# x^T and the branch outputs keep high and low parts side by side, so one 512-column matmul serves both

## The chip, the cores and the metric

The kernel runs on one core of a Trainium2 chip. The metric is the time of one execution in microseconds of device time, the median of three runs. The profile is one execution recorded by the hardware profiler.

## The reference

Two layers of a streaming encoder over 256 tokens (T) of 1024 channels (D). In each layer x passes through four residual steps, each closed by a layer norm:

```
x = LN(a x + 0.5 swiglu_1(x))            swiglu(x) = (silu(x Wg) * (x Wu)) Wd,  2816 hidden columns
x = LN(a x + mixer(x))
x = LN(a x + 0.5 swiglu_2(x))
x = LN(a x + sigmoid(x Wgate + b) * (p Wproj))
```

The mixer projects x once to the inputs of three branches (a recurrent unit RG-LRU, a gated linear attention GLA, a forgetting attention FoX) and to three gates of 1024 columns. Each branch ends in a product of its 512-column output with a branch weight, the three results are gated and added, and a last 1024x1024 product closes the mixer. All of it is float32.

## The kernel before

**Precision.** A float32 product is made of three matmuls of a shorter type (fp32r). Each operand is split in a high part (a ScalarE copy) and a low part (VectorE, the value minus the high part), and the three products high·high, low·high and high·low are summed in one PSUM bank.

**Weights.** 440 pieces of up to 128x1024 are loaded by SP's DMA queue in the order of their use. ScalarE makes `whi` (line 194), VectorE (or GpSimd at some places) makes `wlo` (line 195). Eight pieces, in the feed-forward phases up to 13, are held split, and further ones wait in four raw tiles. A piece is split as soon as one is freed by its last matmul, so the split of a later piece stands on ScalarE's and VectorE's queues behind each unit of work.

**Two kinds of product.** `mm_tok` (lines 288 to 298) holds x^T blocks stationary and moves up to 512 weight columns. `mm_feat` (lines 300 to 310) holds 128x128 of the weights stationary and moves x^T, 256 columns (all tokens): per block one matmul with `XH` on the high weights (line 308), one with `XL` on the high weights (309), one with `XH` on the low weights (310). The output is feature-major, 128 channels by 256 tokens, and two such outputs lie side by side in one bank. A unit of `feat` is 256 columns: two pieces, 16 triples of matmuls. A unit of `branch` has 8 triples, with the branch output `yh`/`yl` moving. Over both layers there are 118 units of `feat` (the first gate chunk of each layer's first feed-forward step counted as one, although it is written out) and 24 of `branch`: 118 x 16 + 24 x 8 = 2080 triples.

**PSUM.** All products take their banks in turn from one pool `ps` of eight 2 KB banks. Who takes a bank waits for the last reader of the tile that had it.

**Order.** Nothing is scheduled at run time: every engine executes its queue in the order in which the program issues it. A feed-forward step runs over 11 chunks of 256 hidden columns: gate unit, silu (ScalarE, from the bank), up unit, product of both (VectorE, from the bank), split into `hh` and `hl`; the down product of a chunk follows two chunks later (`LAG`), and the last two stand at the end. In the mixer the units follow one another while chains of small operations (the recurrent unit, decays, attention) advance one step per unit. Near its start stand, in this order, two units `v` (FoX values, `mm_tok`, copied from their banks by ScalarE at line 553), between them the RG-LRU gates (PE line 667, sigmoids on ScalarE line 671) and `gla_states` (PE line 718). At its end come the third branch's units; each gets its gate factor (VectorE `w<-w,ps`), is added to `mg` and split into `XH` and `XL`, and the closing product (`merge_out`) reads these.

Of the kernel before, what the change touches and what calls it, by code (L numbers as in the profile page):

```python
# [30 lines left out]
# Weight pieces held split: always, and further ones in the feed-forward phases; raw pieces; work tiles.  # L31
# [25 lines left out]
# A group of attention heads starts at every so many units of the merge.  # L57
# [8 lines left out]
def weight_units():  # L66
    """Weight blocks in the order in which the kernel uses them.

    (key, array, index, row 0, rows, column 0, columns, cut): a unit comes in two pieces, cut by rows or by columns."""
# [65 lines left out]
# per-channel vectors of the RG-LRU, feature-major  # L135
# [17 lines left out]
class Weights:  # L153
    """Weight pieces, loaded and split in two float32r parts ahead of their use."""
# [21 lines left out]
    def prefetch(self, n=1, lo=None, cuts=1, between=lambda i: None):  # L176
        """Split up to n more pieces, as far as there is room."""
        for _ in range(n):
            where = self.room()
            if where is None:  # L180
                return False
            key, _, _, _, rows, _, cols, off = PIECES[self.next]
            kt = rows // P
            raw = self.raw.tile([P, PCAP], F32, tag="raw", name=f"raw{self.next}")
            pool = self.extra if where == "extra" else self.main
            hi, lw = (pool.tile([P, PCAP], F32R, tag=x, bufs=R_EXTRA if where == "extra" else R_MAIN, name=f"{x}{self.next}") for x in ("whi", "wlo"))
            hi, lw, raw = (x[:, :kt * cols] for x in (hi, lw, raw))
            src = self.src[off:off + rows * cols].rearrange("(p n) -> p n", p=P)
            m = kt * cols // cuts
            for i in range(cuts):  # L190
                between(i)
                c = slice(i * m, (i + 1) * m)
                self.nc.sync.dma_start(raw[:, c], src[:, c])
                self.nc.scalar.activation(hi[:, c], raw[:, c], AF.Copy)  # L194
                (lo or self.nc.vector).tensor_tensor(out=lw[:, c], in0=raw[:, c], in1=hi[:, c].bitcast(F32), op=ALU.subtract)  # L195
            self.live[key] = [x.rearrange("p (k n) -> p k n", k=kt) for x in (hi, lw)] + [where]
            self.used[where] += 1
            self.next += 1
        return True
# [12 lines left out]
class Chains:  # L212
    """Chains of operations, each a generator, that advance by one step at a time."""
# [11 lines left out]
def build(tc, a, out):  # L225
# [10 lines left out]
    psp = pool("ps", 8, space=PSUM)  # L236
# [8 lines left out]
    def ps():  # L245
        return psp.tile([P, 512], F32, tag="ps", name=nm("ps"))

# [27 lines left out]
    XH = const.tile([P, KD, T], F32R, name="XH")  # L275
    XL = const.tile([P, KD, T], F32R, name="XL")
# [11 lines left out]
    def mm_tok(o, t, w, k0, start, stop, lh=None, ll=None):  # L288
        """o[tokens of tile t, columns] += x^T blocks (stationary) with a piece (moving)."""
        lh, ll = (XH, XL) if lh is None else (lh, ll)  # L290
        hi, lo = w
        kt = hi.shape[1]
        c = slice(t * P, (t + 1) * P)
        for kk in range(kt):
            k = k0 + kk
            TE.matmul(o, lhsT=lh[:, k, c], rhs=hi[:, kk, :], start=start and kk == 0, stop=False)  # L296
            TE.matmul(o, lhsT=lh[:, k, c], rhs=lo[:, kk, :], start=False, stop=False)  # L297
            TE.matmul(o, lhsT=ll[:, k, c], rhs=hi[:, kk, :], start=False, stop=stop and kk == kt - 1)  # L298

    def mm_feat(o, w, col, k0=0, start=True, stop=True, rh=None, rl=None):  # L300
        """o[128 columns of a piece, all tokens] += piece^T (stationary) with x^T (moving)."""
        rh, rl = (XH, XL) if rh is None else (rh, rl)
# [3 lines left out]
        for kk in range(kt):  # L306
            k = k0 + kk
            TE.matmul(o, lhsT=hi[:, kk, c], rhs=rh[:, k, :], start=start and kk == 0, stop=False)  # L308
            TE.matmul(o, lhsT=hi[:, kk, c], rhs=rl[:, k, :], start=False, stop=False)  # L309
            TE.matmul(o, lhsT=lo[:, kk, c], rhs=rh[:, k, :], start=False, stop=stop and kk == kt - 1)  # L310

    def feat(key):
        """256 columns of a product, feature-major, of a unit cut by columns."""
        o = ps()
        for i in range(2):
            mm_feat(o[:, i * T:(i + 1) * T], W.get(key, i), 0)
            W.free(key, i)
        return o

# [11 lines left out]
    class Norm:  # L331
        """Layer norm of tile t of 2 ALPHA x + an addend that comes in column blocks."""
# [14 lines left out]
        def finish(self, gb, cuts=((0, 512), (512, 512)), last=False):  # L347
            """Normalizes; returns what turns the halves feature-major."""
# [25 lines left out]
    def to_feat(y, hi, lo):  # L374
        """hi, lo [128, 4, 128] of the transpose of y [128, 512]."""
# [5 lines left out]
    def steps(work_list, at=(), turn=(), ahead="", inserts={}):  # L381
        """Runs the steps: after step at[n], turn[n]; after step i, a piece split ahead by engine ahead[i]."""
# [11 lines left out]
    def ffn(l, f, ln, hp, turn):  # L394
# [19 lines left out]
        if not first:  # L414
            ht(0), ht(1)

            def up_tok(t, c):
                st = {}

                def step(x, i):  # L420
                    if not st:
                        st["o"] = ps()
# [27 lines left out]
        for c in range(0 if first else 2, NCH):  # L450
            if first and c == 0:
                og = [ps() for _ in range(2)]
                for i in range(2):
                    w = W.get((l, f, "g", c), i)
                    for k in range(4):
                        for j in range(2):
                            mm_feat(og[j][:, :T], [x[:, k:k + 1, :] for x in w], j * P, 4 * i + k, i == 0 and k == 0, i == 1 and k == 3)
                    W.free((l, f, "g", c), i)
            else:
                og = feat((l, f, "g", c))  # L460
            s = work()
            while late:
                late.pop()()
            if isinstance(og, list):
                for j in range(2):
                    S.activation(s[:, j * T:(j + 1) * T], og[j][:, :T], AF.Silu)
            else:
                S.activation(s, og, AF.Silu)
# [30 lines left out]
    def mixer(l, turn):  # L499
# [15 lines left out]
        # columns that are needed token-major  # L515
        acc = {}

        def b_piece(g, t, h, i):
            n = PB[g + 1] - PB[g]
            if (g, t) not in acc:  # L520
                acc[g, t] = ps()
# [33 lines left out]
        def abs_log1p(z, n):  # L555
            """Room for log(sigmoid(z)) = min(z, 0) - log(1 + exp(-|z|)), and that logarithm."""
# [6 lines left out]
        # Each step of these chains needs what earlier steps made, so that no engine waits long.  # L563
        # GLA: decayed keys and chunk decays
# [37 lines left out]
        # FoX: cumulative log forget gates, in three exact bfloat16 parts, transposed  # L602
# [32 lines left out]
        def yt():  # L635
            return [mt([P, 4, T], F32R, x, 2) for x in ("yh", "yl")]

        # RG-LRU
# [21 lines left out]
        def lru(i):  # L660
# [18 lines left out]
            # 1 - a^2 = -tanh(log a) (1 + a^2)  # L679
# [10 lines left out]
            hi, lo = (flat(x[:, 2 * i:2 * i + 2, :]) for x in ya)  # L690
            S.activation(hi, xc, AF.Copy)
            yield
            tt(lo, xc, hi.bitcast(F32), ALU.subtract)

        # head by head, the rows of the other head of the pair zero
# [11 lines left out]
        # GLA: states and outputs  # L707
# [26 lines left out]
        def gla_gate():  # L734
            """silu(r) * norm_g, without its factor of one half."""
# [11 lines left out]
        def gla_out():  # L747
# [25 lines left out]
            for t in range(2):  # L773
                to_feat(sq[t], yb[0][:, :, t * P:(t + 1) * P], yb[1][:, :, t * P:(t + 1) * P])
                yield

        # FoX: attention, in groups of heads that share a PSUM bank
        def fox_attend(t, g):
# [41 lines left out]
            if (g + 1) * nh == NH:  # L820
                if t == 0:
                    fox["y"] = yt()
                split(*(x[:, :, tk] for x in fox["y"]), oy.rearrange("p (h c) -> p h c", h=4))

        # merge: gates (1 + tanh(x / 2)), twice the sigmoid; the factor of two goes into the norm
# [3 lines left out]
        def gate(b, i):  # L829
            o = feat((l, f"gt{b}", i))  # L830
            s = work()
            S.activation(s, o, AF.Tanh, scale=0.5)
            ss[i] = s

        def merge(b, h, q, o):
# [10 lines left out]
            if b == 2:  # L846
                yield
                f = 4 * h + 2 * q
                split(flat(XH[:, f:f + 2, :]), flat(XL[:, f:f + 2, :]), m)

        def branch(b, h, y):
            for q in range(2):
                key = (l, "br", b, h)
                o = ps()
                w = W.get(key, q)
                for j in range(2):
                    mm_feat(o[:, js[j]], w, j * P, rh=y[0], rl=y[1])
                chains.add(merge(b, h, q, o))
# [75 lines left out]
    def ple(l, turn, last):  # L934
# [4 lines left out]
        for t in range(2):  # L939
            for n in range(2):  # L940
                o = ps()
# [34 lines left out]
        def last_step(q):  # L976
            """The last 512 columns in two blocks, so that little is left after the last product."""
# [32 lines left out]
    def lru_constants():  # L1010
        # -8 softplus(-lambda), with log1p(e) = 2 atanh(e / (2 + e))
# [22 lines left out]
    def x_part(k):  # L1034
        s = raws[k // 4][:, (k % 4) * 256:(k % 4 + 2) * 256]
        load(s, a["xT"][:, k * 256:(k + 2) * 256])
        split(flat(XH[:, k:k + 2, :]), flat(XL[:, k:k + 2, :]), s)
# [82 lines left out]
```

## Time and profile before

| | |
|---|---|
| median of 3 runs | 1336.01 us (1334.59 to 1336.84) |
| span of the profiled execution | 1332.8 us |
| mean granted TensorE clock | 0.996 |
| PE busy | 1308.0 us, 98% |
| VectorE busy | 834.6 us, 63% |
| ScalarE busy | 663.3 us, 50% |
| GpSimd busy | 106.2 us, 8% |
| DMA | 246.17 MB, mean 185 GB/s |

The span is that of the recorded instructions; the time of a run is some 3.2 us longer. A row of the timeline gives the start and the duration in us, engine, line, operation, the tiles out<-in, the shape, how many instructions it groups, and in brackets the idle time before it and what ended it. Matmuls are pipelined: their recorded durations overlap, so what one costs is read from the distance between starts.

### The profile page before, as it was taken

Reading aid. Unit: us, or ns where it says so; the run is one execution under the profiler, and the core shown is the slowest. Engines: PE = TensorE matmul, PEld = TensorE weight load, DVE = VectorE, ACT = ScalarE, POOL = GpSimd, SP = SyncE. Lnnn points to the kernel's source line nnn. Section 1 sums busy time; section 2 is a strip of 40 time slices with the busy share of each in tenths; the row PEclk is TensorE's granted clock in tenths of the full one; section 3 lists DMA queues with packets and bytes.
Section 4 is the critical chain, followed back from the end, with each engine's and each line's share of the span. In section 5 each row is a group of like instructions: output and inputs, shape, how many; then the busy total and the mean of one; then the engine's idle time right before and its main releaser. Section 6 shows DMA issues by size and latency. Waiting matters only on the chain. (4 is left out here: it accounts for less than half of the span.)

```text
span 1332.8 us, 22835 instructions
## 1 busy us (share of the span) xinstructions
PE 1308.0 (98%) x9492; PEld 1231.9 (92%) x9492; DVE 834.6 (63%) x992; ACT 663.3 (50%) x869; POOL 106.2 (8%) x69
## 2 busy tenths in 40 slices
PE   8999999999999999999999999999999999999997
PEld 8999999999999999998799999899999989999986
DVE  6665567675657755557775555676755587555576
ACT  6554436965445344454344445279654444444441
POOL 0000001000001400001320000200000022000021
PEclk9999999999999999999999999999999999999998
DMA  8855636445466365574456567454554554656732
GB/s 269 289 198 190 243 127 229 160 159 167 150 190 204 129 193 188 188 239 164 174 191 187 190 185 239 157 184 160 183 160 145 194 187 150 194 188 185 251 128 78
DMA packets 70215, 246.17 MB, mean 185 GB/s; under 512 B 8160, under 2 KB 8672, under 8 KB 70112
## 3 DMA queue, kind: packets, MB, share of 16 engines
q1 hardware_dynamic: 69824, 244.33, 56.6%
q8 instruction: 74, 1.21, 0.4%
q10 hardware_dynamic: 288, 0.39, 0.1%
q14 instruction: 29, 0.24, 0.1%
HBM read 243.64 MB, written 1.05 MB: 184 GB/s over the span
## 5 line engine op out<-in xcount | busy, mean ns | idle before, releaser
L195 DVE TENSOR_TENSOR wlo<-raw,whi 128x1024 fp32r<-128x1024 f32 (+3 forms) x419 | 513.5, 1235 | 393.3 <-ACT whi L194 392.1
L194 ACT ACTIVATE whi<-raw 128x1024 fp32r<-128x1024 f32 (+3 forms) x442 | 459.5, 1047 | 443.8 <-PE ps L309 258.7
L308 PE MATMUL ps<-XH,whi 128*128 128x256 f32 x1888 | 535.1, 283 | 5.7 <-ACT whi L194 5.7
L309 PE MATMUL ps<-XL,whi 128*128 128x256 f32 x1888 | 531.0, 281 | 0.0
L310 PE MATMUL ps<-XH,wlo 128*128 128x256 f32 x1888 | 531.0, 281 | 0.0
L308 PEld LDWEIGHTS ps<-XH,whi 128*128 128x128 f32 x1888 | 357.2, 189 | 8.1 <-ACT whi L194 5.7
L309 PEld LDWEIGHTS ps<-XL,whi 128*128 128x128 f32 x1888 | 357.0, 189 | 1.4
L310 PEld LDWEIGHTS ps<-XH,wlo 128*128 128x128 f32 x1888 | 357.2, 189 | 0.2 <-DVE wlo L195 0.2
L296 PE MATMUL ps<-whi,XH 128*128 128x256 f32 (+3 forms) x488 | 162.3, 333 | 0.0
L297 PE MATMUL ps<-wlo,XH 128*128 128x256 f32 (+3 forms) x488 | 159.2, 326 | 0.0
L298 PE MATMUL ps<-whi,XL 128*128 128x256 f32 (+3 forms) x488 | 158.4, 325 | 0.0
L296 PE MATMUL ps<-whi,hh 128*128 128x512 f32 x368 | 144.5, 393 | 0.0
L298 PE MATMUL ps<-whi,hl 128*128 128x512 f32 x368 | 143.6, 390 | 0.0
L297 PE MATMUL ps<-wlo,hh 128*128 128x512 f32 x368 | 143.4, 390 | 0.0
L298 PEld LDWEIGHTS ps<-whi,XL 128*128 128x128 f32 x488 | 92.1, 189 | 6.6
L296 PEld LDWEIGHTS ps<-whi,XH 128*128 128x128 f32 x488 | 91.9, 188 | 6.8 <-ACT tm L553 0.3
L297 PEld LDWEIGHTS ps<-wlo,XH 128*128 128x128 f32 x488 | 92.3, 189 | 5.9
L298 PEld LDWEIGHTS ps<-whi,hl 128*128 128x128 f32 x368 | 69.1, 188 | 15.0
L297 PEld LDWEIGHTS ps<-wlo,hh 128*128 128x128 f32 x368 | 69.3, 188 | 13.0
L296 PEld LDWEIGHTS ps<-whi,hh 128*128 128x128 f32 x368 | 69.1, 188 | 12.8
L354 POOL TENSOR_TENSOR s<-s,mhalf 128x1 f32<-128x1 f32 x16 | 15.6, 976 | 792.5 <-DVE s L266 792.5
L195 POOL TENSOR_TENSOR wlo<-raw,whi 128x1024 fp32r<-128x1024 f32 (+1 forms) x23 | 58.1, 2534 | 32.9 <-ACT whi L194 29.3
(161 smaller groups left out, 1053.4 us busy)
## 6 DMA issues: line engine op xcount, KB each, us to landing
raw<-in_wu SPq DMA_DIRECT2D x414, 512.0 KB, 4.1
gb<-in_lnp SPq DMA_DIRECT2D x16, 512.0 KB, 6.5
raw<-in_wu SPq DMA_DIRECT2D x16, 436.0 KB, 4.3
raw<-in_wu SPq DMA_DIRECT2D x8, 432.0 KB, 4.5
xr<-in_xT SPq DMA_DIRECT2D x4, 256.0 KB, 4.6
raw<-in_wu SPq DMA_DIRECT2D x4, 256.0 KB, 5.1
XR<-in_x SPq DMA_DIRECT2D x1, 1024.0 KB, 7.0
wa<-in_lru SPq DMA_DIRECT2D x2, 512.0 KB, 3.8
```

What stands on the lines that cost most here:

```text
L194: self.nc.scalar.activation(hi[:, c], raw[:, c], AF.Copy)
L195: (lo or self.nc.vector).tensor_tensor(out=lw[:, c], in0=raw[:, c], in1=hi[:, c].bitcast(F32), op=ALU.subtract)
L296: TE.matmul(o, lhsT=lh[:, k, c], rhs=hi[:, kk, :], start=start and kk == 0, stop=False)
L297: TE.matmul(o, lhsT=lh[:, k, c], rhs=lo[:, kk, :], start=False, stop=False)
L298: TE.matmul(o, lhsT=ll[:, k, c], rhs=hi[:, kk, :], start=False, stop=stop and kk == kt - 1)
L308: TE.matmul(o, lhsT=hi[:, kk, c], rhs=rh[:, k, :], start=start and kk == 0, stop=False)
L309: TE.matmul(o, lhsT=hi[:, kk, c], rhs=rl[:, k, :], start=False, stop=False)
L310: TE.matmul(o, lhsT=lo[:, kk, c], rhs=rh[:, k, :], start=False, stop=stop and kk == kt - 1)
L354: G.tensor_tensor(out=rs, in0=rs, in1=mhalf[:, 0:1], op=ALU.pow)
```

## The change

XH and XL become two views of one tile `XX` [128, 8, 2, 256], and `yh` and `yl` of one tile `y` [128, 4, 2, 256], so that for a block k the high and low parts are 512 columns in a row. `mm_feat` sends both through the high weights in one 512-column matmul; the 256-column matmul with the low weights adds to the second half. The first half of a bank then holds high·high, the second half the two small products. A unit of 256 columns takes two banks (a tile `pp`) in place of one. `summed` adds the halves: ScalarE copies the second halves to SBUF, VectorE adds the first halves. What read the bank before (silu, tanh, the product, the split, the gate factor) reads the sum in SBUF now. The pool `ps` has four banks, and `pp` has two tiles of two.

```diff
-    psp = pool("ps", 8, space=PSUM)
+    psp = pool("ps", 4, space=PSUM)
+    ppp = pool("pp", 2, space=PSUM)
...
-    XH = const.tile([P, KD, T], F32R, name="XH")
-    XL = const.tile([P, KD, T], F32R, name="XL")
+    XX = const.tile([P, KD, 2, T], F32R, name="XX")
+    XH, XL = XX[:, :, 0, :], XX[:, :, 1, :]
...
         for kk in range(kt):
             k = k0 + kk
-            TE.matmul(o, lhsT=hi[:, kk, c], rhs=rh[:, k, :], start=start and kk == 0, stop=False)
-            TE.matmul(o, lhsT=hi[:, kk, c], rhs=rl[:, k, :], start=False, stop=False)
-            TE.matmul(o, lhsT=lo[:, kk, c], rhs=rh[:, k, :], start=False, stop=stop and kk == kt - 1)
+            both = rhs[:, k].rearrange("p s c -> p (s c)")
+            last = stop and kk == kt - 1
+            if not last:
+                TE.matmul(o, lhsT=hi[:, kk, c], rhs=both, start=start and kk == 0, stop=False)
+            TE.matmul(o[:, T:], lhsT=lo[:, kk, c], rhs=rhs[:, k, 0, :], start=False, stop=False)
+            if last:
+                TE.matmul(o, lhsT=hi[:, kk, c], rhs=both, start=False, stop=True)
+
+    def summed(o):
+        s = work()
+        v = s.rearrange("p (j c) -> p j c", j=2)
+        S.activation(v, o[:, :, T:], AF.Copy)
+        tt(v, o[:, :, :T], v, ALU.add)
+        return s
 
     def feat(key):
-        o = ps()
+        o = pp()
         for i in range(2):
-            mm_feat(o[:, i * T:(i + 1) * T], W.get(key, i), 0)
+            mm_feat(o[:, i, :], W.get(key, i), 0)
+            if i:
+                s = summed(o)
             W.free(key, i)
-        return o
+        return s
...
-            S.activation(s, og, AF.Silu)
+            S.activation(s, s, AF.Silu)
...
-                chains.add(merge(b, h, q, o))
+                chains.add(merge(b, h, q, summed(o)))
```

Some other products (the first two chunks' token-major part of a later feed-forward step, two groups of the mixer's token-major columns, the embedding product) take pairs of `pp` banks in place of `ps` banks; their arithmetic is the same.

On ScalarE, around the copies of the first `v` unit (`tm<-ps` at the end of the piece), the queue was this (L658 are the gelus of two `ay` units, L683 and L560 belong to chains):

```order
L560 ACTIVATE w_2598<-w_2598 128x16
L194 ACTIVATE whi_2632<-raw_2631 128x1024
L194 ACTIVATE whi_2662<-raw_2661 128x1024
L658 ACT_TABLE_LOAD
L658 ACTIVATE w_2667<-ps_2606 128x512
L683 ACT_TABLE_LOAD
L683 ACTIVATE w_2498<-w_2498 128x512
L194 ACTIVATE whi_2702<-raw_2701 128x1024
L194 ACTIVATE whi_2732<-raw_2731 128x1024
L553 ACTIVATE tm_2072<-ps_2675 128x256
L553 ACTIVATE tm_2072<-ps_2676 128x256
L671 ACT_TABLE_LOAD
```

The same place of the changed kernel (L681 is the gelu, L706 and L582 the chains, L575 the copies of `v`, L694 the sigmoids):

```order
L582 ACTIVATE w_2258<-w_2258 128x16
L194 ACTIVATE whi_2284<-raw_2283 128x1024
L327 ACTIVATE w_2305<-pp_2266 128x512
L194 ACTIVATE whi_2309<-raw_2308 128x1024
L681 ACT_TABLE_LOAD
L681 ACTIVATE w_2314<-w_2305 128x512
L706 ACT_TABLE_LOAD
L706 ACTIVATE w_2171<-w_2171 128x512
L194 ACTIVATE whi_2349<-raw_2348 128x1024
L194 ACTIVATE whi_2379<-raw_2378 128x1024
L575 ACTIVATE tm_1775<-ps_2322 128x256
L575 ACTIVATE tm_1775<-ps_2323 128x256
```

The copy of the `ay` unit's second halves (L327) is new there; another stands before the first `ay` unit's gelu. On PE the instructions that follow the first `v` unit are the same in both kernels; in the changed one they stand as below, with the semaphores they wait for (L690 the RG-LRU gates, L742 `gla_states`, L301 the second `v` unit):

```order
L690 MATMUL ps_2393<-w_2075,wa_1771 128x256 [waits Activation_49]
L690 MATMUL ps_2396<-w_2075,wa_1771 128x256 [waits Activation_49]
L742 MATMUL ps_2407<-tm_1775,w_2316 64x128 [waits DVE_49,Activation_49]
L742 MATMUL ps_2407<-tm_1775,w_2316 64x128 x3
L742 MATMUL ps_2408<-tm_1775,w_2318 64x128 [waits DVE_49,Activation_49]
L742 MATMUL ps_2408<-tm_1775,w_2318 64x128 x3
L301 MATMUL ps_2437<-whi_2150,XX 128x256 [waits Activation_49]
L301 MATMUL ps_2438<-whi_2150,XX 128x256 [waits Activation_49]
```

With four banks in turn, `ps_2407` and `ps_2408` take the banks of `ps_2322` and `ps_2323` (the first `v` unit), and `ps_2437` and `ps_2438` those of `ps_2393` and `ps_2396`. On VectorE, before the closing product of the mixer, the queue was (L263 the gate factors, `XL<-mg` the low parts that the closing product reads):

```order
L263 SCALAR_TENSOR_TENSOR w_4344<-w_4344,ps_4518 128x512
L195 TENSOR_TENSOR wlo_4547<-raw_4545,whi_4546 128x1024
L260 TENSOR_TENSOR XL<-mg_3426,XH 128x512
L263 SCALAR_TENSOR_TENSOR w_4414<-w_4414,ps_4551 128x512
L195 TENSOR_TENSOR wlo_4582<-raw_4580,whi_4581 128x1024
L260 TENSOR_TENSOR XL<-mg_3426,XH 128x512
L845 TENSOR_TENSOR mg_3677<-mg_3677,w_4414 128x512
```

and is now (`w<-pp,w` are the adds of `summed`):

```order
L264 TENSOR_TENSOR w_3903<-pp_3886,w_3903 128x512
L267 SCALAR_TENSOR_TENSOR w_3737<-w_3737,w_3903 128x512
L195 TENSOR_TENSOR wlo_3910<-raw_3908,whi_3909 128x1024
L264 TENSOR_TENSOR w_3931<-pp_3914,w_3931 128x512
L264 TENSOR_TENSOR XX<-mg_2975,XX 128x2x256
L267 SCALAR_TENSOR_TENSOR w_3793<-w_3793,w_3931 128x512
L195 TENSOR_TENSOR wlo_3940<-raw_3938,whi_3939 128x1024
L264 TENSOR_TENSOR w_3961<-pp_3944,w_3961 128x512
L264 TENSOR_TENSOR XX<-mg_2975,XX 128x2x256
L868 TENSOR_TENSOR mg_3188<-mg_3188,w_3793 128x512
```

One add per branch unit stands ahead of the gate factor and of the split that is due there.

## Rows read from the trace of the kernel before

**Rows 1.** Page, part 1: busy time of each engine, share, instructions.
```profile
PE 1308.0 (98%) x9492; PEld 1231.9 (92%) x9492; DVE 834.6 (63%) x992; ACT 663.3 (50%) x869; POOL 106.2 (8%) x69
```
**Rows 2.** Waits over the whole span: engine, line, releaser, total us, times, longest.
```profile
ACT whi L194 <- PE ps L309: 258.7, 152, 4.0
```
**Rows 3.** Timeline of PE, feed-forward: a down product, then an up unit (256 columns).
```profile
42.66 0.28 PE L310 MATMUL ps<-XH,wlo 128*128 128x256 f32 x1
42.78 0.39 PE L296 MATMUL ps<-whi,hh 128*128 128x512 f32 x1
...
48.01 0.39 PE L298 MATMUL ps<-whi,hl 128*128 128x512 f32 x1
48.23 0.28 PE L308 MATMUL ps<-XH,whi 128*128 128x256 f32 x1
...
98.83 0.28 PE L308 MATMUL ps<-XH,whi 128*128 128x256 f32 x1
...
104.53 0.28 PE L308 MATMUL ps<-XH,whi 128*128 128x256 f32 x1
```
**Rows 4.** Timeline of PE in the closing product of the mixer.
```profile
417.59 0.40 PE L296 MATMUL ps<-whi,XH 128*128 128x512 f32 x1
...
423.90 0.39 PE L296 MATMUL ps<-whi,XH 128*128 128x512 f32 x1
...
425.30 0.39 PE L296 MATMUL ps<-whi,XH 128*128 128x512 f32 x1
```
**Rows 5.** Groups by shape, ScalarE and VectorE: busy us, mean ns, idle before.
```profile
L832 ACT ACTIVATE w<-ps 128x512 f32<-128x512 f32 x24 | 14.0, 582 | 0.0
L260 DVE TENSOR_TENSOR w<-w,ps 128x512 f32<-128x512 f32 x38 | 25.8, 680 | 0.0
```
**Rows 6.** Timeline of PE after the first v unit.
```profile
259.12 1.97 PE L718 MATMUL ps<-tm,w 128*64 128x128 f32 x32
261.02 0.39 PE L296 MATMUL ps<-whi,XH 128*128 128x256 f32 x1
```
**Rows 7.** Timeline of ScalarE, same place.
```profile
238.41 1.28 ACT L671 ACT_TABLE_LOAD   x1
...
258.65 1.99 ACT L194 ACTIVATE whi<-raw 128x1024 fp32r<-128x1024 f32 x2
260.55 0.64 ACT L553 ACTIVATE tm<-ps 128x256 f32<-128x256 f32 x2
...
262.50 1.57 ACT L671 ACTIVATE w<-ps,vec 128x256 f32<-128x256 f32 x4
```
**Rows 8.** Timeline of PE at a norm, then windows (PE to POOL busy, PEclk, DMA).
```profile
660.86 1.11 PE L378 MATMUL ps<-cf,XR 128*128 128x128 f32 x4 [2.56 <-DVE XR L263]
660.00:665.00 5.00, 4.14 (x17) 3.52 (x18) 4.24 (x7) 2.90 (x4) 1.45 (x2) 0.66 0.33 105
```
**Rows 9.** Timeline near the start: ScalarE, VectorE, PE.
```profile
34.08 1.06 ACT L194 ACTIVATE whi<-raw 128x1024 fp32r<-128x1024 f32 x1 [0.97 <-DMA raw<-in_wu]
37.04 1.22 DVE L195 TENSOR_TENSOR wlo<-raw,whi 128x1024 fp32r<-128x1024 f32 x1 [0.64 <-ACT whi L194]
37.09 0.28 PE L308 MATMUL ps<-XH,whi 128*128 128x256 f32 x1
```
**Rows 10.** Timeline of VectorE at the end of the mixer.
```profile
410.25 2.22 DVE L195 TENSOR_TENSOR wlo<-raw,whi 128x1024 fp32r<-128x1024 f32 x1 [0.29 <-ACT whi L194]
...
414.24 1.79 DVE L260 TENSOR_TENSOR XL<-mg,XH 128x512 fp32r<-128x512 f32 x1
...
417.68 0.68 DVE L260 TENSOR_TENSOR XL<-mg,XH 128x512 fp32r<-128x512 f32 x1
```
**Rows 11.** Timeline at the end of the last feed-forward step, VectorE and PE.
```profile
1279.06 0.68 DVE L260 TENSOR_TENSOR w<-w,ps 128x512 f32<-128x512 f32 x1
1280.44 1.29 DVE L260 TENSOR_TENSOR hl<-w,hh 128x512 fp32r<-128x512 f32 x2 [0.70 <-ACT hh L269]
1280.87 0.39 PE L296 MATMUL ps<-whi,hh 128*128 128x512 f32 x1
```

More of the change, by code (lines that the diff above doesn't have):

```diff
@@ L246, in ps, with pp @@
         return psp.tile([P, 512], F32, tag="ps", name=nm("ps"))
+    def pp():
+        return ppp.tile([P, 2, 512], F32, tag="pp", name=nm("pp"))
     def work(n=512, dt=F32):
@@ L298, in mm_tok, with mm_feat @@
             TE.matmul(o, lhsT=ll[:, k, c], rhs=hi[:, kk, :], start=False, stop=stop and kk == kt - 1)
-    def mm_feat(o, w, col, k0=0, start=True, stop=True, rh=None, rl=None):
-        rh, rl = (XH, XL) if rh is None else (rh, rl)
+    def mm_feat(o, w, col, k0=0, start=True, stop=True, rhs=None):
+        rhs = XX if rhs is None else rhs
         hi, lo = w
@@ L415, in ffn @@
             ht(0), ht(1)
+            banks = {}
             def up_tok(t, c):
@@ L421, in step @@
                     if not st:
-                        st["o"] = ps()
+                        if c == 0:
+                            banks[t] = pp()
+                        st["o"] = banks[t][:, c, :]
                     key = (l, f, "gu"[x], c)
@@ L451, in ffn @@
             if first and c == 0:
-                og = [ps() for _ in range(2)]
+                og = pp()
                 for i in range(2):
@@ L456, in ffn @@
                         for j in range(2):
-                            mm_feat(og[j][:, :T], [x[:, k:k + 1, :] for x in w], j * P, 4 * i + k, i == 0 and k == 0, i == 1 and k == 3)
+                            mm_feat(og[:, j, :], [x[:, k:k + 1, :] for x in w], j * P, 4 * i + k, i == 0 and k == 0, i == 1 and k == 3)
                     W.free((l, f, "g", c), i)
+                s = summed(og)
             else:
-                og = feat((l, f, "g", c))
-            s = work()
+                s = feat((l, f, "g", c))
             while late:
                 late.pop()()
[L464 to L467, printed above, removed]
-                S.activation(s, og, AF.Silu)
+            S.activation(s, s, AF.Silu)
             ou = feat((l, f, "u", c))
@@ L513, in mixer @@
         kT = tm[:, :, TM_V:TM_V + 512].rearrange("p i (h c) -> p i h c", h=4)
-        acc = {}
+        acc, banks = {}, {}
         def b_piece(g, t, h, i):
@@ L520, in b_piece @@
             if (g, t) not in acc:
-                acc[g, t] = ps()
+                if g == 0:
+                    banks[t] = pp()
+                acc[g, t] = banks[t][:, g, :] if g < 2 else ps()
             key = (l, "b", g, h)
@@ L635, in yt @@
         def yt():
-            return [mt([P, 4, T], F32R, x, 2) for x in ("yh", "yl")]
+            y = mt([P, 4, 2, T], F32R, "y", 2)
+            return y, y[:, :, 0, :], y[:, :, 1, :]
         ya = yt()
@@ L689, in lru @@
             yield
-            hi, lo = (flat(x[:, 2 * i:2 * i + 2, :]) for x in ya)
-            S.activation(hi, xc, AF.Copy)
+            hi, lo = (x[:, 2 * i:2 * i + 2, :] for x in ya[1:])
+            xc3 = xc.rearrange("p (j c) -> p j c", j=2)
+            S.activation(hi, xc3, AF.Copy)
             yield
-            tt(lo, xc, hi.bitcast(F32), ALU.subtract)
+            tt(lo, xc3, hi.bitcast(F32), ALU.subtract)
         def unit_q(key, dst, h0):
@@ L773, in gla_out @@
             for t in range(2):
-                to_feat(sq[t], yb[0][:, :, t * P:(t + 1) * P], yb[1][:, :, t * P:(t + 1) * P])
+                to_feat(sq[t], yb[1][:, :, t * P:(t + 1) * P], yb[2][:, :, t * P:(t + 1) * P])
                 yield
@@ L822, in fox_attend @@
                     fox["y"] = yt()
-                split(*(x[:, :, tk] for x in fox["y"]), oy.rearrange("p (h c) -> p h c", h=4))
+                split(*(x[:, :, tk] for x in fox["y"][1:]), oy.rearrange("p (h c) -> p h c", h=4))
         merged = []
@@ L829, in gate @@
         def gate(b, i):
-            o = feat((l, f"gt{b}", i))
-            s = work()
-            S.activation(s, o, AF.Tanh, scale=0.5)
+            s = feat((l, f"gt{b}", i))
+            S.activation(s, s, AF.Tanh, scale=0.5)
             ss[i] = s
@@ L848, in merge @@
                 f = 4 * h + 2 * q
-                split(flat(XH[:, f:f + 2, :]), flat(XL[:, f:f + 2, :]), m)
+                split(XH[:, f:f + 2, :], XL[:, f:f + 2, :], m.rearrange("p (j c) -> p j c", j=2))
         def branch(b, h, y):
@@ L853, in branch @@
                 key = (l, "br", b, h)
-                o = ps()
+                o = pp()
                 w = W.get(key, q)
                 for j in range(2):
-                    mm_feat(o[:, js[j]], w, j * P, rh=y[0], rl=y[1])
-                chains.add(merge(b, h, q, o))
+                    mm_feat(o[:, j, :], w, j * P, rhs=y[0])
+                chains.add(merge(b, h, q, summed(o)))
                 W.free(key, q)
@@ L940, in ple @@
             for n in range(2):
-                o = ps()
+                if n == 0:
+                    banks = pp()
+                o = banks[:, n, :]
                 for i in range(2):
@@ L1036, in x_part @@
         load(s, a["xT"][:, k * 256:(k + 2) * 256])
-        split(flat(XH[:, k:k + 2, :]), flat(XL[:, k:k + 2, :]), s)
+        split(XH[:, k:k + 2, :], XL[:, k:k + 2, :], s.rearrange("p (j c) -> p j c", j=2))
     for k in (0, 4):
```

## The prediction

> **What bounds the kernel.** I read the page's busy times first. PE works 1308.0 of 1332.8 us, 98% of the span; VectorE and ScalarE are busy 63% and 50% [rows 1]. The reader is to see one engine that is never out of work for long. The table of waits says why the others are not behind it: ScalarE's split of a weight piece waits 258.7 us in 152 places for line 309, that is for PE to free a piece [rows 2]. Weights are there before PE asks, so almost everything PE saves comes off the end, and every stall put into PE's queue goes onto it. Then the timeline, for what a matmul costs and for the places where another engine is only just ahead of PE. The span is 1332.8 us, the median 1336.01; the sum below is made on the span and carried over to the median with the same 3.2 us around it.
>
> **A. The matmuls (PE).** An `up` unit is 48 matmuls of 256 columns, from 98.83 to 104.53: 5.70 us, 118.75 ns each [rows 3]. The 24 matmuls of 512 columns of a down product run from 42.78 to 48.23: 227 ns each [rows 3]. A triple was 3 x 118.75 = 356.3 ns and becomes 227 + 118.75 = 345.9 ns: 10.4 ns less. There are 2080 triples (118 x 16 + 24 x 8): 2080 x 10.4 = **-21.6 us**, 0.166 us in each unit of `feat`. No stretch of the trace alternates the two shapes, so the bounds come from their borders. A 256-column matmul followed by a 512-column one took 42.78 - 42.66 = 0.12, the reverse 48.23 - 48.01 = 0.22 [rows 3]; at the trace's resolution of 0.01 a pair of 0.343 would be possible, -27 us. In the mixer's closing product six 512-column matmuls took 425.30 - 423.90 = 1.40 us, 233 ns each [rows 4]; a pair of 0.352 gives -9 us. I take 227, from the down products, because they stand among these units.
>
> A rule speaks for a smaller gain. The rows make a matmul's cost beyond its columns about 10 ns: two of 256 cost 237.5, one of 512 costs 227 [rows 3]. The Trainium skill (TensorE: Matmul & The Clock Gate, section Back-to-back issue gap) gives the gap of a single matmul as its columns at full clock plus about 2.5 ns. By that each avoided matmul would save 2.5 ns, 5.2 us in all, and with the stalls below the time would be 1349 us, which is where rival 2 lies. The rows disagree with it here, and the sum goes by the rows.
>
> **B. The two `v` units of each mixer (a new wait for banks).** With eight banks, the two tiles of `gla_states` had banks that were long free. With four they have those of the `v` unit just before, and PE must wait for the two copies at line 553. PE started `gla_states` at 259.12 [rows 6]; the copies started at 260.55 and took 0.64 together [rows 7]. That alone would be a stall of 1.8 us. It becomes longer at both ends. ScalarE works without a gap from 238.41 to there (no row of the stretch shows idle time [rows 7]), and two copies of `summed` now stand in that stretch (the two `ay` units), 0.58 each by a copy of this shape [rows 5]; less 0.33 us by which two earlier units are shorter, the first copy ends at 261.4 + 0.36 = 261.7. PE gets there four units' savings earlier, at 259.12 - 0.66 = 258.46. Stall 3.3 us. The second `v` unit then needs the banks of the RG-LRU gates, whose sigmoids started at 262.50, two per bank at 1.57 / 4 each [rows 7]: freed at 262.50 + 0.83 + 0.79 = 264.1, against PE at 263.7: another 0.4. So **+3.7 us** in a mixer, +7.4 in both. Lower bound: 1.8 per mixer, if the copies of `summed` find room; upper 5. Behind the waiting matmul stands everything on PE, so nothing hides it.
>
> A gap of this length has a price of its own here. At a norm PE was idle for 2.56 us before 660.86, and in the window after it the granted clock was 0.66 [rows 8], that is PE ran for most of it at the lower of its two levels, 1.2 GHz. Over these 5 us 1 - 0.66 of 5.0 = 1.7 us of clock were missing. I count that half for each mixer: **+1.7 us**; bounds 0 and 3.4.
>
> **C. The start.** The first 40 us are bound by loads: ScalarE's splits wait for DMA there (0.97 before 34.08) [rows 9], and PE has no weights in hand. The up unit that starts at 37.09 needs a `pp` tile that the add of an earlier unit frees, and that add stands on VectorE behind a `wlo` that ends at 37.04 + 1.22 = 38.26 [rows 9]. With the add's 0.68 [rows 5] PE waits until 39.0 instead of 37.09 less five units' 0.83 = 36.3: **+2.7 us**. Lower bound 0 (the loads give it back later, since PE would have waited for weights anyway), upper 4.
>
> **D. End of the mixer.** PE began the closing product at 417.59 [rows 4], VectorE wrote the first low parts from 414.24 and the second at 417.68 [rows 10]. They ended at 416.03 and 418.36; the matmuls that read them are the third of PE's first six and of its next six, at 418.06 and 419.46 by 0.233 each, 2.0 and 1.1 us later. VectorE works there without a gap from 410.25 on. Now four adds of 0.68 stand in that stretch, one for each branch unit, three of them before the second of these writes. The first block is late by some 0.5 us, the second by another 1.8; the later blocks have more room. **+2.3 us** in a mixer, +4.6 in both; bounds 0 (the weight splits among them give way) and 2.7 each (all four adds).
>
> **E. End of the feed-forward steps.** The last product's `hl` is just in time: the multiplication ran at 1279.06, the split at 1280.44, and PE started the next to last down product at 1280.87 [rows 11] and needs its `hl` two matmuls later, at 1281.3; the first of the two splits ended at 1281.1, 0.2 before. Now copy and add (0.58 + 0.68, [rows 5]) stand in front of it, and PE comes two units' savings (0.33) earlier. The fourth step pays 1.26 - 0.2 + 0.33 = 1.4 us, the other three about 0.2 each since there more stands between: **+2.0 us**; bounds 0 and 5 (all four pay all).
>
> **Costed at nothing.** ScalarE's 142 copies (82 us) and VectorE's 142 adds (97 us): over the span both have more than a third of their time idle [rows 1], and VectorE's busy share becomes (834.6 + 97) / 1332.8 = 70%. The cover is the room that PE's own length leaves; it is gone where A to E say. A `pp` tile in the steady part is used again one whole unit of 5.5 us later, against 0.58 + 0.68 and at most two splits of about 1.2 in front. The smaller count of matmul and weight-load instructions also costs DMA nothing.
>
> **Sum.** -21.6 + 7.4 + 1.7 + 2.7 + 4.6 + 2.0 = -3.2 us. On the profiled span that is 1329.6, on the median **1333 us**. 0.2% or 2.7 us is about what a measurement of this kernel can tell from no change.
>
> **Rivals.**
> (1) *The gain comes whole and the stalls stay small.* For it: A rests on long stretches of rows, while B to E are added up from queues that may shift; the lower bounds of B to E are 3.6 + 0 + 0 + 0 + 0. Against: in B the row shows PE ready 1.4 us before the copies even without the change's copies. Price: -21.6 + 3.6 to + 10, 1318 to 1325 us.
> (2) *Slower: the four banks at the `v` units decide.* One mechanism: PE waits for ScalarE's queue there, ScalarE is later than I walked it (its queue is solid, and table loads of 1.28 us stand in it), the wait reaches 5 us in each mixer and the clock falls to its lower level after both: 2 x (5 + 1.7) = 13.4 in place of 9.1. It decides if the matmuls save little, since with 233 ns for the long one the gain is 9 us: -9 + 13.4 + 9.3 = +13.7, 1350 us. With the gain halfway, at 15 us, it is +8, 1344. The point from which it is slower is a gain under the sum of the stalls, 18 to 23 us.
> (3) *The matmul step doesn't shrink.* If a 512-column matmul that alternates with a 256-column one costs two of 256, A is zero and the stalls are all that is left: 1336 + 18 = 1354. Against: 227 ns at the border of the two shapes [rows 3].
>
> **Chances.** My sum 0.47, spread 1328 to 1339; rival 1 0.25; rival 2 0.24; rival 3 0.04. The sum's own spread lies to 0.44 beyond -2.7, to 0.38 within and to 0.18 slower. Faster: 0.25 + 0.47 x 0.44 = 0.46; same: 0.47 x 0.38 + 0.06 of rival 2 near its edge = 0.24; slower: 0.47 x 0.18 + 0.18 + 0.04 = 0.30. The range for 8 in 10 is 1319 to 1346.
>
> **What would show it.** A: starts of consecutive 512- and 256-column matmuls in an `up` unit 0.346 apart, and such a unit in 5.53 us. B: `gla_states` on PE with about 3.3 us of idle time released by ScalarE's `tm<-ps`, in both mixers, and a window after it with a granted clock under 0.9. C: an up unit near 36 us waiting for VectorE's add. D: idle before a matmul of the closing product, released by VectorE's `XX<-mg`. E: idle before the last down product, released by `hl`. The prediction is wrong if PE's stalls outside the norms sum to under 8 or over 25 us, or if the pair is not between 0.343 and 0.352.

## The result, and the profile after

The changed kernel takes 1374.37 us (median, 1373.39 to 1378.06), the kernel before 1335.48 on the same chip: a ratio of 1.0296 [1.0281, 1.0311], 39 us slower. The forecast was 1333, with a range that ended at 1346. The profiled execution has a span of 1372.4 us.

The first part of the page, to be laid beside [rows 1]:

```profile
PE 1309.0 (95%) x7412; PEld 1135.0 (83%) x7412; DVE 914.5 (67%) x1134; ACT 734.3 (54%) x1010; POOL 116.6 (8%) x69
```

PE has 2080 matmuls less and is no less busy: the recorded durations overlap, and part of them ran at the lower clock. What the reader is to see is the share, 95% in place of 98%. The table of PE's waits shows what it waited for (before, its only rows were 9.4 us at the norms and 5.7 us for the first weights):

```profile
PE pp L301 <- DVE w L264: 25.6, 6, 8.1
PE ps L742 <- DVE wlo L195: 8.1, 2, 4.2
PE pp L318 <- DVE XX L264: 5.9, 1, 5.9
PE pp L301 <- ACT tm L549: 4.5, 4, 1.6
PE ps L399 <- DVE XR L267: 3.7, 5, 1.1
PE pp L301 <- ACT w L970: 2.7, 4, 0.7
PE pp L318 <- DVE w L264: 1.4, 2, 1.2
PE ps L303 <- DVE XX L264: 0.8, 2, 0.4
PE pp L303 <- DVE XX L264: 0.6, 1, 0.6
PE ps L301 <- ACT hh L273: 0.5, 2, 0.2
```

The largest row was in none of my terms. Line 301 is `mm_tok`, here the token-major products with which each later feed-forward step starts (tile `pp`), and 25.6 us fall in six places. PE's timeline at the first of the long ones:

```profile
452.98 0.28 PE L303 MATMUL pp<-whi,XX 128*128 128x256 f32 x1
458.99 0.58 PE L301 MATMUL pp<-whi,XX 128*128 128x256 f32 x1 [5.73 <-DVE w L264]
459.37 0.41 PE L302 MATMUL pp<-wlo,XX 128*128 128x256 f32 x1
459.58 0.41 PE L303 MATMUL pp<-whi,XX 128*128 128x256 f32 x1
```

and VectorE's in the same stretch:

```profile
453.01 5.59 DVE L267 SCALAR_TENSOR_TENSOR XR<-z,s,gb 128x512 f32<-128x512 f32 x2
458.52 0.41 DVE L264 TENSOR_TENSOR w<-w,pp 128x256 f32<-128x256 f32 x1
```

PE has finished chunk 0 of token tile 0 and wants to begin chunk 1 at 453.1. It begins when VectorE has read chunk 0's bank (the product with the gate, at 458.52), and that read stands behind two operations of the norm of 2.8 us each. Chunk 1 is written to another bank, but the two banks are one tile: `up_tok` keeps the two chunks of a token tile in one `pp`. The order of PE's instructions has the wait. Both rows are from the changed kernel: the first is a matmul of chunk 0 with its second weight piece, the second the first matmul of chunk 1.

```order
L301 MATMUL pp_4185<-whi_4003,XX 128x256 [waits Activation_49]
L301 MATMUL pp_4185<-whi_4040,XX 128x256 [waits DVE_49]
```

In the kernel before, chunk 1 went into a `ps` bank of its own. So this is no behaviour of PSUM but a semaphore in the program: who writes one bank of a tile waits for the readers of the whole tile.

The windows that follow stalls, the first a short one of 1.62 us at the `b` columns, the others those at `gla_states` and at the starts of the feed-forward steps (columns as in [rows 8], the clock is the third number from the end):

```profile
212.00:217.00 5.00, 5.00 (x25) 4.75 (x26) 3.01 (x4) 2.78 (x3) 0.00 (x0) 1.00 0.82 272
264.00:269.00 5.00, 4.32 (x40) 4.15 (x41) 4.93 (x9) 4.95 (x11) 0.00 (x0) 0.66 0.59 187
459.00:464.00 5.00, 5.00 (x30) 5.00 (x31) 0.00 (x0) 0.01 (x1) 0.00 (x0) 0.68 0.29 105
691.00:696.00 5.00, 4.83 (x29) 4.83 (x30) 0.12 (x1) 0.00 (x0) 0.00 (x0) 0.67 0.30 105
710.00:716.00 6.00, 5.82 (x31) 5.82 (x32) 1.69 (x3) 1.06 (x1) 0.00 (x0) 0.60 0.47 160
951.00:956.00 5.00, 4.81 (x37) 4.49 (x38) 4.93 (x11) 4.95 (x10) 0.00 (x0) 0.50 0.63 206
1147.00:1152.00 5.00, 5.00 (x26) 5.00 (x26) 0.00 (x0) 0.00 (x0) 0.00 (x0) 0.53 0.24 94
```

Behind each of the long ones PE works for some us at a granted clock between 0.50 and 0.68; matmuls of 256 columns start 0.21 apart there (459.37 to 459.58 above) against 0.12 at the full clock.

The matmuls did shrink. An up unit that answers to [rows 3], and the two matmuls of its first block:

```profile
99.40 0.40 PE L318 MATMUL pp<-XX,whi 128*128 128x512 f32 x1
99.63 0.28 PE L319 MATMUL pp<-XX,wlo 128*128 128x256 f32 x1
99.75 0.39 PE L318 MATMUL pp<-XX,whi 128*128 128x512 f32 x1
...
104.97 0.39 PE L318 MATMUL pp<-XX,whi 128*128 128x512 f32 x1
```

Sixteen pairs take 104.97 - 99.40 = 5.57 us, 0.348 a pair, against 5.70 before.

Cutting both timelines at the same places, some 390 changes of PE's work (a stage ends where PE turns to another kind of matmul) gives where the 39.6 us of span come from:

| stages | longer by (us) |
|---|---|
| starts of the three later feed-forward steps (paired banks) | 7.4 + 8.6 + 6.9 + 8.0, less 2.7 given back behind them |
| first b columns of the mixers, embedding products (paired banks) | 1.0 + 1.8 + 0.8 + 1.9, 1.9 + 2.0 |
| RG-LRU gates, `gla_states`, second v unit | 5.3 and 7.1 |
| closing products of the mixers | 0.8 + 0.8 |
| ends of the feed-forward steps (three that stand out) | 0.8 + 0.7 + 0.4 |
| first stage (start) | 1.2 |
| all other units of `feat` and `branch` | -13.4 |
| the rest (norms, where PE now comes later) | -1.7 |

### The profile page after: what moved, and what is told of

The parts are those of the page before. It is cut to its first block, busy times and chain, and to the rows that moved or that the text cites. A ratio compares the mean times of both kernels' runs of the same rounds, so it can differ in the third digit from the quotient of the medians.

```text
span 1372.4 us, 18932 instructions
## 1 busy us (share of the span) xinstructions
PE 1309.0 (95%) x7412; PEld 1135.0 (83%) x7412; DVE 914.5 (67%) x1134; ACT 734.3 (54%) x1010; POOL 116.6 (8%) x69
## 5 line engine op out<-in xcount | busy, mean ns | idle before, releaser
L318 PE MATMUL pp<-XX,whi 128*128 128x512 f32 x1652 | 592.1, 396 | 7.3 <-DVE XX L264 5.9
L319 PE MATMUL pp<-XX,wlo 128*128 128x256 f32 x1888 | 491.3, 280 | 0.0
L319 PEld LDWEIGHTS pp<-XX,wlo 128*128 128x128 f32 x1888 | 356.3, 189 | 18.6 <-DVE wlo L195 0.7
L318 PEld LDWEIGHTS pp<-XX,whi 128*128 128x128 f32 x1652 | 311.5, 189 | 70.7 <-ACT whi L194 5.8
L327 ACT ACTIVATE w<-pp 128x512 f32<-128x512 f32 x142 | 84.7, 596 | 184.2 <-PE pp L321 184.1
L264 DVE TENSOR_TENSOR w<-pp,w 128x512 f32<-128x512 f32 x142 | 98.0, 690 | 102.5 <-ACT w L327 102.5
L301 PE MATMUL ps<-whi,hh 128*128 128x512 f32 x352 | 138.2, 393 | 0.5 <-ACT hh L273 0.5
L301 PE MATMUL pp<-whi,XX 128*128 128x256 f32 (+1 forms) x256 | 83.2, 325 | 30.1 <-DVE w L264 25.6
L321 PE MATMUL pp<-XX,whi 128*128 128x512 f32 x236 | 92.8, 394 | 0.0
L301 PE MATMUL ps<-whi,XX 128*128 128x512 f32 (+2 forms) x232 | 83.7, 361 | 0.0
L303 PE MATMUL ps<-whi,XX 128*128 128x512 f32 (+2 forms) x232 | 82.1, 354 | 0.8 <-DVE XX L264 0.8
L302 PE MATMUL ps<-wlo,XX 128*128 128x512 f32 (+2 forms) x232 | 81.7, 352 | 0.0
L303 PE MATMUL pp<-whi,XX 128*128 128x256 f32 (+1 forms) x256 | 80.2, 313 | 0.6 <-DVE XX L264 0.6
L302 PE MATMUL pp<-wlo,XX 128*128 128x256 f32 (+1 forms) x256 | 80.2, 313 | 0.0
L301 PEld LDWEIGHTS pp<-whi,XX 128*128 128x128 f32 x256 | 51.7, 202 | 33.6 <-DVE w L264 26.9
L301 PEld LDWEIGHTS ps<-whi,hh 128*128 128x128 f32 x352 | 66.1, 188 | 13.7 <-ACT hh L273 1.7
```

Of the source, the lines that this page charges most:

```text
L264: return V.tensor_tensor(out=out, in0=in0, in1=in1, op=op)
L318: TE.matmul(o, lhsT=hi[:, kk, c], rhs=both, start=start and kk == 0, stop=False)
L319: TE.matmul(o[:, T:], lhsT=lo[:, kk, c], rhs=rhs[:, k, 0, :], start=False, stop=False)
L321: TE.matmul(o, lhsT=hi[:, kk, c], rhs=both, start=False, stop=True)
L327: S.activation(v, o[:, :, T:], AF.Copy)
```

## The experiments

Theory 1 after the result: a wait for paired banks, put there by how the tiles are used. Its rival, theory 2: the copies and adds of the sums fill ScalarE's and VectorE's queues, and whatever wait is taken away comes back at the next place.

**e1: the pair holds a chunk, not a token tile.**

```diff
-                        if c == 0:
-                            banks[t] = pp()
-                        st["o"] = banks[t][:, c, :]
+                        if t == 0:
+                            banks[c] = pp()
+                        st["o"] = banks[c][:, t, :]
```

> One edit in the changed kernel: at the start of a later feed-forward step the token-major products of chunk c, tiles 0 and 1, share a pp tile (one per chunk), where the two chunks of one token tile shared it. Theory 1 (paired banks): a matmul into one bank of a pair waits for every reader of the other bank, and the reader here (VectorE's product of chunk 0) stands behind the norm's two 2.8 us operations; the stages there were longer by 7.4, 8.6, 6.9 and 8.0 us less 3 us given back behind them, so about -28 us: 1346 us, and no wait of PE line 301 on VectorE's product. Theory 2 (full queues): the copies and adds of the sums make ScalarE and VectorE late, and the wait only moves to the transposes behind; above 1365 us.

Measured: 1344.24 us, ratio to the kernel before 1.0068 [1.0051, 1.0085]; 30.1 us less than the changed kernel for three lines that change no operation. The same matmul now waits for nothing on VectorE:

```order
L301 MATMUL pp_4249<-whi_4040,XX 128x256 [waits PE_49]
```

The row `pp L301 <- DVE w L264` is gone from PE's waits. The transposes behind (line 399, at the norms) wait somewhat longer than the 3.7 us of the changed kernel, since PE comes to them earlier, but not longer than the 9.4 us of the kernel before:

```profile
PE ps L399 <- DVE XR L267: 7.5, 6, 2.2
```

So little of the wait moved there, and theory 2 falls for these 30 us.

**e2: the same for the two other users of pairs.** The edit is of the same kind in `b_piece` (`banks[g][:, t, :]`) and at the embedding product (`banks[n][:, t, :]`).

> The edit of e1, and the same for the two other users of paired tiles (the first two groups of the mixer's token-major columns and the embedding product: a pair holds the two token tiles of a group or column half). Theory 1: the longer stages there (1.0, 1.8, 0.8, 1.9 us in the mixers' starts, 1.9 and 2.0 us at the embedding products) go as well, about -8 us against e1: 1338 us. Theory 2: no change against e1.

Measured: 1338.51 us, 1.0021 [1.0012, 1.0030]; -5.7 us. In the profiled runs the four stages in the mixers and the two at the embedding products are 9.5 us shorter; some 5 come back in other stages (2.2 at the embedding gate of layer 0, 1.5 at the RG-LRU gates, 0.9 at the start).

**e3: the v units take a pair.**

```diff
         def unit_v(i):
-            o = [ps() for _ in range(2)]
+            o = pp()
+            o = [o[:, t, :] for t in range(2)]
```

> The edits of e2, and the two v units of each mixer take a pair of banks (both token tiles) from pp in place of two banks of ps, so that gla_states and the RG-LRU gates have four banks of ps for themselves. Theory 1 (four banks): the stalls of 5.4 and 7.1 us at gla_states and the second v unit go, -11 to -12 us against e2: 1327 us, faster than the kernel before by the matmuls' gain of some 14 us less 5 us at the ends of the feed-forward steps. Theory 2: ScalarE is late by its own queue, and PE then waits elsewhere in that place; less than -4 us.

Measured: 1329.96 us, 0.9959 [0.9944, 0.9974]: 0.4% faster than the kernel before. Against e2 it is -8.6, where -11 to -12 was expected; the stages at the v units are 5.4 and 6.5 us shorter as expected, but the first stage is 1.6 us longer, in code that was not edited. The row for `ps` at `gla_states`, 9.4 us in e2, becomes:

```profile
PE ps L743 <- DVE w L267: 1.2, 2, 1.0
```

**e4: the kernel before, with the changed kernel's banks alone.** Three 256-column matmuls, no sums; pools and pairs as in the changed kernel, a unit using one bank of a pair.

```diff
-    psp = pool("ps", 8, space=PSUM)
+    psp = pool("ps", 4, space=PSUM)
+    ppp = pool("pp", 2, space=PSUM)
...
-        o = ps()
+        o = pp()[:, 0, :]
...
-                        st["o"] = ps()
+                        if c == 0:
+                            banks[t] = pp()
+                        st["o"] = banks[t][:, c, :]
...
```

> The kernel before with the changed kernel's PSUM pools (four single banks and two pairs) and its use of the pairs, but with three 256-column matmuls and no sums (a unit takes one bank of a pair). Theory 1: the waits for paired banks come with the pools alone: 1336 + 28 + 8 + 4 to 8 at the v units (without the copies of the sums the stall there is 1.8 us and the clock after it) = 1376 to 1380 us, as slow as the changed kernel although it has none of its added work. Theory 2: 1336 to 1345 us, since neither copies nor adds are there.

Measured: 1379.84 us, 1.0331 [1.0316, 1.0347]. Without any of the added work it is 5 us slower than the changed kernel, and the waits of PE that cost most in the changed kernel are there again (the second row is that for the first weights, which every kernel here has):

```profile
PE pp L300 <- DVE w L264: 25.9, 6, 8.1
PE pp L312 <- ACT whi L194: 6.7, 1, 6.7
PE pp L300 <- ACT tm L538: 4.5, 4, 1.6
PE ps L729 <- ACT tm L564: 3.6, 2, 1.8
```

So the banks alone make the loss. The 3.6 us at `gla_states` (line 729) are 1.8 in each mixer, the value that the prediction worked out for the stall without the copies of the sums; the changed kernel, with these copies, has 3.9 and 4.2. There theory 2 holds in part: the added work lengthened a wait that the banks had made.

**e5: the same with the pairs used as in e3.**

> The kernel before with the pools of four single banks and two pairs, used as in e3 (pairs by chunk, group and column half, v units in a pair), but with three 256-column matmuls and no sums. Theory 1: with no reader in the other half of a pair that a matmul must wait for, the smaller pools cost nothing: 1335 to 1338 us, 42 us less than e4. What e3 has less than this (about 6 us) is then the matmuls' gain of some 15 us less what the sums cost at the start, at the end of each feed-forward step and at the end of each mixer. Theory 2: the smaller pools or the 256-column triples are slow for another reason; above 1345 us.

Measured: 1338.52 us, 1.0024 [1.0016, 1.0033]; -41.3 against e4. The pools alone still cost 3 us, and the first stage is 3.0 us longer. There are no sums here: PE waits at the start for those who read a pair's bank directly, at 21.19 for the silu (line 475) and at 28.13 for the product:

```profile
PE pp L312 <- ACT w L475: 1.3, 1, 1.3
PE pp L312 <- DVE w L264: 1.0, 1, 1.0
```

So at the start, too, two pairs are enough to make PE wait, whoever their reader is. Laid beside e3, which has the same banks, e5 separates the matmuls: the units of `feat` and `branch` take 12.8 us less in e3, the closing products and the ends of the feed-forward steps 2 to 3 us more, and the RG-LRU gates and `gla_states` 1.6 us more.

**e6: in the first four chunks both pieces of a unit are freed after its sum.**

```diff
-    def feat(key):
+    def feat(key, late=False):
...
             if i:
                 s = summed(o)
-            W.free(key, i)
+                if late:
+                    W.free(key, 0)
+            if i or not late:
+                W.free(key, i)
...
-                s = feat((l, f, "g", c))
+                s = feat((l, f, "g", c), first and c < 4)
...
-            ou = feat((l, f, "u", c))
+            ou = feat((l, f, "u", c), first and c < 4)
```

What it is to take away, in e3: ScalarE's split waits for a load, VectorE's split waits for that one, and the add stands behind it. PE waits for the add, 1.13 us before 40.03.

```profile
37.05 1.06 ACT L194 ACTIVATE whi<-raw 128x1024 fp32r<-128x1024 f32 x1 [1.16 <-DMA raw<-in_wu]
38.15 1.23 DVE L195 TENSOR_TENSOR wlo<-raw,whi 128x1024 fp32r<-128x1024 f32 x1 [0.99 <-ACT whi L194]
39.29 0.68 DVE L264 TENSOR_TENSOR w<-pp,w 128x512 f32<-128x512 f32 x1
```

> e3, and in the first four chunks of the first feed-forward step both pieces of a unit are freed after its sum is issued, so the sum stands on ScalarE's and VectorE's queues ahead of the two weight splits that freeing the first piece starts. Theory A: at the start the sum is late because it stands behind splits that wait for DMA; PE's waits there (0.5, 1.2 and 1.5 us for VectorE's add) go and the first stage, which is 2.9 us longer than in the kernel before, is 2 to 3 us shorter: 1327.5 us. Theory B: PE is bound by the loads at the start, and waits for weights instead: 1330 us, or more as pieces are asked for later.

Measured: 1326.71 us, 0.9941 [0.9928, 0.9954], the fastest kernel with the whole computation. The first stage is 3.4 us shorter than in e3. Theory A: what held PE at the start was not the loads but the sum's place behind splits that wait for loads. All that PE still waits for:

```profile
PE ps L402 <- DVE XR L267: 9.6, 9, 3.3
PE pp L318 <- ACT whi L194: 5.8, 1, 5.8
PE ps L746 <- DVE w L267: 2.2, 2, 1.2
PE ps L303 <- DVE XX L264: 0.8, 2, 0.4
PE ps L655 <- DVE fcat L649: 0.3, 2, 0.2
PE ps L301 <- ACT hh L273: 0.3, 1, 0.3
```

The first two are the norms and the first weights, as before the change.

**e7: no adds.** `summed` without its second line, on e3, so that high·high is left out of all that follows.

> e3 without VectorE's 142 adds: the sum is ScalarE's copy of the second halves alone, so the high-high product is left out of what follows. If the adds are hidden except at the three places named (start, ends of the feed-forward steps, ends of the mixers, 2.9 + 2.2 + 1.6 us, of which the add is a bit over half): 1325.5 to 1327 us. If VectorE's 98 us of adds cost throughout by delaying the splits of the weights: under 1322 us.

Measured: 1323.42 us, 0.9907 [0.9894, 0.9920]; -6.5 against e3, between the two ranges: a gain 2 us larger than the first allowed, and not the one under 1322. Half is the first stage (-3.2); of the rest the RG-LRU gates before `gla_states` of layer 0 have -1.1, the closing products -0.4 each and the embedding gate of layer 0 -1.0. VectorE's 98 us of adds cost 6.5 us, not 98, and e6 has 3.2 of these back with the adds in.

**e8: the last up unit summed in halves.** On e6; each half of 256 columns takes a bank of a pair of its own.

```diff
+            if c == NCH - 1:
+                hi, lo = ht(c)
+                for i in range(2):
+                    o = pp()
+                    mm_feat(o[:, 0, :], W.get((l, f, "u", c), i), 0)
+                    v, g = work(T), s[:, i * T:(i + 1) * T]
+                    S.activation(v, o[:, 0, T:], AF.Copy)
+                    tt(v, o[:, 0, :T], v, ALU.add)
+                    tt(g, g, v, ALU.mult)
+                    split(hi[:, i, :], lo[:, i, :], g)
+                    W.free((l, f, "u", c), i)
+                continue
...
```

> e6, and the last up unit of each feed-forward step is summed, multiplied and split in two halves of 256 columns, the halves in different pairs of banks, so that the first half is done while PE works on the second. The chain behind PE's last matmul of the unit has five operations of half the length. Theory A: the down products that now wait for that chain (0.4 to 0.8 us in each of the four steps) do not wait: -2 to -3 us against e6, 1325 us, and no wait of PE for hh. Theory B: those waits come from the down products' own first use after the sums' queue, not from the chain's length: no change against e6.

Measured: 1334.25 us, 0.9994 [0.9982, 1.0005], 7.5 us more than e6: neither theory. There was little to win: in e6 PE waits for `hh` in one place only, 0.3 us, and not 0.4 to 0.8 in each step. That wait did go, but the second half now takes the pair of the gate unit half a unit after that unit's end. PE, and VectorE in the same stretch:

```profile
606.06 0.40 PE L321 MATMUL pp<-XX,whi 128*128 128x512 f32 x1
608.43 0.50 PE L318 MATMUL pp<-XX,whi 128*128 128x512 f32 x1 [1.97 <-DVE w L264]
```

```profile
606.55 1.23 DVE L195 TENSOR_TENSOR wlo<-raw,whi 128x1024 fp32r<-128x1024 f32 x1 [1.80 <-ACT whi L194]
607.70 0.68 DVE L264 TENSOR_TENSOR w<-pp,w 128x512 f32<-128x512 f32 x1
```

The gate unit's add ends at 608.38, behind a split of a weight piece, and PE waits for it: 5.7 us in the four steps. It also bounds the cover that I counted on: with two pairs a whole unit of 5.6 us between two uses hides the sum here, half a unit does not.

## Why the prediction was wrong

**What failed.** "Costed at nothing" was the step. Of the paired tiles the prediction weighed only those of the sums, where a pair is used again one whole unit later. That other users of pairs still have a reader waiting on one bank when the other is to be written was left out, although the diff has it (`banks[t][:, c, :]`). These cost 36 us: 30.1 by e1 and 5.7 by e2; e4, which has the same pairs without the sums, has the same waits. The lists of waits in the order of the changed kernel showed the semaphore before any run; I had walked them at `gla_states` only. With this term the sum would have been -3 + 36 = +33.

**A, the matmuls.** Predicted -21.6 (0.346 a pair, bounds 0.343 to 0.352). Measured 0.348 in the feed-forward steps: 8.2 ns less than a triple, -17 for 2080. The stages of `feat` and `branch`, without the first, show only 12.8 to 13.4. No wait is behind this: in most of the mixer's units a triple had cost 0.352, not the 0.356 of [rows 3] (16 triples from 214.95 to 220.58 before, 16 pairs from 216.84 to 222.41 after, 5.64 and 5.56 us). Right in kind and inside the bounds, 5 us too large by the pair and 8 by the stages. By the rule of the Trainium skill (TensorE: Matmul & The Clock Gate, section Back-to-back issue gap) it would have been -5.2, an estimate from its 2.5 ns a matmul; the trace after, with 5 to 8 ns a triple, does not agree with it either.

**B, the v units.** Predicted +7.4 and 1.7 for the clock, 9.1. Measured 12.4: waits of 3.9 and 4.2 us, then the lower clock, which came after both (0.66 and 0.50), where I had counted it half. The mechanism was right: e3 takes it away with two lines, e4 has it at 1.8 a mixer without the sums. PE's wait, as it stands in the changed kernel, is put down to `wlo`:

```profile
264.68 0.48 PE L742 MATMUL ps<-tm,w 128*64 128x128 f32 x2 [3.94 <-DVE wlo L195]
264.27 0.64 ACT L575 ACTIVATE tm<-ps 128x256 f32<-128x256 f32 x2
```

The copies at line 575 are the releaser: PE starts as the first of the two ends, and in e3, where the `v` unit has banks of its own, the wait is gone.

**C, the start.** Predicted +2.7, measured +1.2 in the changed kernel; in e3 the first stage was 2.9 longer than before, and e6 took 3.4 off it. The place and the reason (an add behind a split that waits for a load) were right for this kernel, but e5 shows that the add is not needed for it: with two pairs and no sums at all the stage is 3.0 longer, as in e3. And the size is not settled: e1, the changed kernel, e2 and e3 have the same code in this stage and take 37.5, 38.3, 38.3 and 40.0 us, the kernel before 37.1.

**D, end of the mixer.** Predicted +4.6, measured +1.6: one wait in each mixer, released by `XX`, at the place that was named.

```profile
424.40 0.39 PE L302 MATMUL ps<-wlo,XX 128*128 128x512 f32 x1
425.21 0.50 PE L303 MATMUL ps<-whi,XX 128*128 128x512 f32 x1 [0.43 <-DVE XX L264]
```

The two starts are 0.81 apart in place of 0.23, and those beside them some 0.1 each longer. I had walked VectorE's queue as it was before, but there is more room in it now: in the 7.4 us ahead of the closing product three splits had taken 4.65 us (one of them 2.22), and two take 2.4.

**E, ends of the feed-forward steps.** Predicted +2.0, measured 1.9 where it stands out, as 0.8 + 0.7 + 0.4, with the smallest in the step to which I had given 1.4: the sum was near by luck.

**The rivals.** The side was that of rival 2 (four single banks decide, 1344 to 1350), and a part of it held: its place was the v units, which gave 12.4 us of the 39 (it said 13.4, with waits of 5 us), and the clock fell after both. But it needed a small gain of the matmuls to come out slower, and the larger part of the loss had another place. The sign of being wrong that I had named, stalls of PE outside the norms above 25 us in sum, came: 44 us, the first weights not counted. Rival 3 fell with the pair at 0.348.

## What to carry to other kernels

A tile of several PSUM banks is one tile to the semaphores: put into it what is written together and read together, and never two things of which one is read late while the other is being written. When a pool shrinks or tiles are merged, go through every user's first write in the order of the changed kernel and ask what that write waits for and what stands ahead of the releaser on its engine. And with a busy engine at 98%, a merge of instructions that saves it 1% is worth as much as the waits it brings allow: the same matmuls lost 39 us with one use of the banks and won 5.6 with another (e3), and 9 with the sums issued earlier at the start as well (e6).

## What the runs showed of the hardware

The stalls of 3.9 to 8.1 us at `gla_states` and at the starts of the feed-forward steps were followed by stretches at a granted clock of 0.50 to 0.68, that is mostly at 1.2 GHz; the one of 1.62 us at the `b` columns by 1.00. So a stall cost more than its length: in `gla_states` itself, whose matmuls took 3.37 us in place of 1.97 [rows 6] in the first mixer, 1.4 and 1.7 us. A 512-column matmul that alternates with a 256-column one costs 0.348 us with it, 2 ns more than the two cost in runs of their own shape [rows 3]. Why the first stage is 1.6 us longer in e3 than in e2, whose code there is the same, stays open.
